# VectorE's order in the up-projections of a two-layer decoder trunk, one core of a Trainium2

## Chip, cores and metric

The kernel runs on one core of one Trainium2 chip. The metric is the time of one launch on the device in microseconds (us), the median of several runs. Its engines are TensorE (PE in the profile; its weight loads PEld), VectorE (DVE), ScalarE (ACT), GpSimd (POOL) and SyncE (SP), which issues all DMAs.

## What is computed

A residual stream `x` of 1024 tokens by 1024 features goes through two layers: gated linear attention and a gated MLP, then differential attention and a second gated MLP. The change concerns the first half of both MLPs:

```python
def conv_ffn(h, w_in, conv_w, conv_b, w_out):
    u = h @ w_in
    up = jnp.pad(u, ((0, 0), (CONV_WIDTH - 1, 0), (0, 0)))
    c = sum(up[:, j:j + S, :] * conv_w[j] for j in range(CONV_WIDTH)) + conv_b
    a, g = jnp.split(c, 2, axis=-1)
    return (jax.nn.silu(g) * a) @ w_out
```

`h` is the stream after an RMSNorm, `w_in` is 1024 by 5632, the convolution has width 3 over positions.

## The kernel before

**Numbers as pairs.** Every float32 operand of a product is split into a rounded part "hi" and the rest "lo" (`halves`, line 205): ScalarE copies hi (line 208), and VectorE subtracts to get lo (`lo_of`, line 117), which it can do only after ScalarE's copy. One 128x128 by 128x512 block product is then three matmuls: hi by hi, lo by hi, hi by lo (lines 909 to 911). An activation's pair is a tile `xp`, a weight's pair a tile `wp`.

**The up-projection.** `ffn` (from line 846, called once for each MLP) makes the 5632 columns in 22 steps `i`, each of one 128-wide block of `a` and one of `g`. A step is seven products instead of eight (a Strassen-Winograd scheme on 2 by 2 quadrants). `product(i, n)` (line 896) takes the weight pair, allots a bank of PSUM (`pf`, eight of them) and issues 12 matmuls: four k, three each. `mid(i, n, o)` (line 857) adds the result into the step's tiles `u`: mostly VectorE additions (line 114), for some n a ScalarE copy. For steps 0 and 1 some of these sums are GpSimd's (`fine(POOL, ...)`).

**Seven forms of the activations.** Each product form n has its own four `xp` tiles. Set "11" and "21" are there when `ffn` starts; "22", "t1", "t2", "t3" and "t4" are made inside it by `factor1` (line 407). The first 14 products go by n = 0, 2, 6, 4, 1, 3, 5 with i = 0 and 1 for each, and between them `factor1` is called after products 1, 2, 4, 6 and 8 (table `WHEN`). For "t1" to "t4" it does, four times over, a subtraction `h<-h` (line 114, VectorE) and then `halves` of the result: ScalarE's hi, VectorE's lo. In the text below products are counted from 0 in TensorE's order, so products 0 to 13 are steps 0 and 1, products 14 to 20 are step 2, and so on; `wp` q is the weight of product q.

**The convolution.** `conv_a(i-1)`, `conv_g0(i-1)` and `conv_g1(i-1)` are issued among the products of step i: a ScalarE start (`conv_0`, line 916), two VectorE multiply-adds of 128x1024 (`conv_1`, tile `c`), a Silu on ScalarE and a VectorE product `c<-c,c`. Step 2 carries the convolutions of steps 0 and 1.

**The weights.** `take` keeps WIN = 4 weight pairs ready ahead of the one taken. The seven weight forms of a step come from sums of its raw blocks (`sums`, line 215, and `pieces`, line 225), made by GpSimd into `wt` and `raw`, then split by `halves` into `wp`.

**Who sets the order.** TensorE, ScalarE and SyncE run in the order in which the Python code issues their instructions (`tc.manual_schedule`). VectorE's and GpSimd's order is set by the tile scheduler, which places an instruction by its own estimate of when its inputs are ready. All five run their own queue in order.

Of the kernel before, what the change touches and what calls it, by code (L numbers as in the profile page):

```python
# [28 lines left out]
NF = DFF // P  # L29
# [3 lines left out]
WIN = 4  # L33
# [4 lines left out]
WHEN = {1: "22", 2: "t1", 4: "t2", 6: "t3", 8: "t4"}  # L38
CV = (2, 3, 4, 5)
# [11 lines left out]
def trunk(  # L51
# [26 lines left out]
    PE, ACT, DVE, POOL = nc.tensor, nc.scalar, nc.vector, nc.gpsimd  # L78
# [10 lines left out]
    def uid(s):  # L89
        count[0] += 1  # L90
        return f"{s}_{count[0]}"
# [7 lines left out]
    def PS(name):  # L99
        return pp.tile([P, 512], F32, tag="p", name=uid(name))  # L100
# [9 lines left out]
    def H(hf):  # L110
        return slice(hf * HALF, (hf + 1) * HALF)

    def tt(eng, o, a, b, op):
        eng.tensor_tensor(out=o, in0=a, in1=b, op=op)  # L114
# [52 lines left out]
    LOADS, AHEAD, WENG = 3, 2, DVE  # L167
# [97 lines left out]
    def take():  # L265
        prefetch(1)
        r = ready.popleft()
        prefetch(AHEAD)
        return r
# [44 lines left out]
    def fine(eng, o, a, b, op):  # L314

        n = o.shape[-1]
        for c in range(0, n, 256 if eng is POOL else n):
            q = slice(c, c + 256 if eng is POOL else n)
            tt(eng, o[:, q], a[:, q], b[:, q], op)
# [181 lines left out]
    nm = Norm(G_ATTN0)  # L501
    X = nm.X
    tps, qps = [PS("pf"), PS("pf")], [PS("pf"), PS("pf")]
    AHEAD, LOADS = 0, 0
# [3 lines left out]
    for d in range(ND):  # L508
# [17 lines left out]
        if d == 5:  # L526
            LOADS = 3
            prefetch(0)
    AHEAD = 2
# [320 lines left out]
    def ffn(l, nm, g):  # L850
        nonlocal AHEAD
        nonlocal LOADS
        F = nm.f
        FS = ("11", "t2", "21", "t3", "t1", "t4", "22")
        up_tiles = {}

        def mid(i, n, o):

            ua, ug = up_tiles[i]
            a1, a2, g1, g2 = (t[:, 2 + q * HALF:2 + (q + 1) * HALF] for t in (ua, ug) for q in range(2))  # L860
            if i < 2:
                if n == 0:
                    ACT.activation(g1, o, AF.Copy)
                elif n == 2:
                    tt(DVE, a1, o, g1, ALU.add)
                elif n == 6:
                    ACT.activation(a2, o, AF.Copy)
                elif n == 4:
                    ACT.activation(g2, o, AF.Copy)
                    tt(DVE, a2, o, a2, ALU.add)  # L870
                elif n == 1:
                    tt(DVE, g1, o, g1, ALU.add)
                    fine(POOL, a2, a2, g1, ALU.add)
                elif n == 3:
                    tt(DVE, g1, o, g1, ALU.add)
                    fine(POOL, g2, g2, g1, ALU.add)
                else:
                    tt(DVE, g1, o, g1, ALU.add)
                return
            if n == 0:  # L880
                ACT.activation(a1, o, AF.Copy)
            elif n == 1:
                tt(DVE, a2, o, a1, ALU.add)
            elif n == 2:
                tt(DVE, a1, o, a1, ALU.add)
            elif n == 3:
                tt(DVE, g1, o, a2, ALU.add)
            elif n == 4:
                tt(DVE, g2, o, g1, ALU.add)
                tt(DVE, a2, o, a2, ALU.add)  # L890
            elif n == 5:
                tt(DVE, g1, o, g1, ALU.add)
            else:
                tt(DVE, a2, o, a2, ALU.add)

        def product(i, n):

            if n == 0:
                ut = [up.tile([P, 1026], F32, tag="u", name=uid("u")) for _ in range(2)]
                for t in ut:  # L900
                    POOL.memset(t[:, 0:2], 0.0)
                up_tiles[i] = ut
            w = take()
            o = PS("pf")
            fs = F[FS[n]]
            for k in range(ND // 2):
                wh, wl = w[:, k * P:(k + 1) * P], w[:, HALF + k * P:HALF + (k + 1) * P]
                xh, xl = fs[k][:, H(0)], fs[k][:, H(1)]
                PE.matmul(o, wh, xh, start=(k == 0), stop=False)  # L909
                PE.matmul(o, wl, xh, start=False, stop=False)  # L910
                PE.matmul(o, wh, xl, start=False, stop=(k == ND // 2 - 1))  # L911
            return o

        def conv_0(f, ut):
            c = U("c")
            ACT.activation(c, ut[:, 2:2 + S], AF.Identity, scale=cv[:, l, f, 2:3], bias=cv[:, l, f, 3:4])  # L916
            return c

        def conv_1(f, ut, c):
            stt(DVE, c, ut[:, 1:1 + S], cv[:, l, f, 1:2], c, ALU.mult, ALU.add)  # L920
            stt(DVE, c, ut[:, 0:S], cv[:, l, f, 0:1], c, ALU.mult, ALU.add)
# [3 lines left out]
        def conv_a(i):  # L925
            ca[i] = conv_0(i, up_tiles[i][0])
            conv_1(i, up_tiles[i][0], ca[i])
            up_tiles[i][0] = None

        def conv_g0(i):  # L930
            cg[i] = conv_0(NF + i, up_tiles[i][1])
            conv_1(NF + i, up_tiles.pop(i)[1], cg[i])

        def conv_g1(i):
            gt = cg.pop(i)
            ACT.activation(gt, gt, AF.Silu)  # L936
            a = ca.pop(i)
            tt(DVE, a, a, gt, ALU.mult)
            ca["m" if i % 2 == 0 else "a"] = a
            if i % 2 == 1:  # L940
                mix(i)
# [3 lines left out]
        def spill_m():  # L945
            for dst, src in spills:
                nc.sync.dma_start(dst, src.rearrange("p (n t) -> p n t", n=2) if len(dst.shape) == 3 else src)
            spills.clear()
# [23 lines left out]
        def load_w(f):  # L972
            t = (O if f % 2 else E)[f // 2] = U("wo")
            nc.sync.dma_start(t, w_out[l, f])

        def load_r(n, j):

            if (n, j) != (0, NJ - 1):
                r = rraw[n, j] = rawtile("tr")
                k = min(2, NJ - j)  # L980
                nc.sync.dma_start(r[:, 0:k * HALF].rearrange("p (e t) -> p e t", e=k), td[l][j // 2][:, SRC[n], 0:k])

        def factors(n, j):

            a, b = ((w[j][:, H(0)], w[j][:, H(1)]) if j in w else (None, None) for w in (E, O))
            if n == 0:
                x = a[0]
            elif n == 1:
                x = U("ws")[:, H(0)]
                tt(DVE, x, a[0], a[1], ALU.subtract)  # L990
            elif n == 2:
                x = a[0]
                tt(DVE, a[1], a[1], b[1], ALU.add)
                tt(DVE, x, a[1], x, ALU.subtract)
            elif n == 3:
                x = a[1]
            elif n == 4:
                x = a[0]
                tt(DVE, x, b[0], x, ALU.subtract)
                del E[j]  # L1000
            elif n == 5:
                x = b[1]
            else:
                x = b[0]
                del O[j]
            lp[n, j] = halves(x, "lp")
            rp[n, j] = halves(rraw[n, j - j % 2][:, H(j % 2)], "rp")
            if j % 2 == 1 or j == NJ - 1:
                del rraw[n, j - j % 2]
# [46 lines left out]
                sink.add(d, sl, ht[d])  # L1056

        AHEAD = WIN
        for k, (n, i) in enumerate((n, i) for n in (0, 2, 6, 4, 1, 3, 5) for i in range(2)):
            o = product(i, n)  # L1060
            if k == 0:
                nm.begin(1)
            if k == 1:
                nm.end(1)
            if k in WHEN:
                nm.factor1(WHEN[k])
            mid(i, n, o)
        for i in range(2, NF):
            for p, n in enumerate(range(7)):
                if i == NF - 1:  # L1070
                    AHEAD, LOADS = min(WIN, 6 - p), 0
                    if p > 0:
                        load_w(2 * p - 2)
                    if p in (3, 5):
                        load_r(0, p - 3)
                    if p > 4:
                        factors(0, p - 5)
                mid(i, n, product(i, n))
                if i == NF - 1:
                    del F[FS[n]]  # L1080
                if i == 2:
                    (conv_a, conv_g0, conv_g1, conv_a, conv_g0, conv_g1, lambda i: spill_m())[p](p // 3)
                    continue
                if p == CV[0]:
                    conv_a(i - 1)
                if p == CV[1]:
                    conv_g0(i - 1)
                if i < NF - 1 and p == CV[2]:
                    conv_g1(i - 1)
                if p == CV[3]:  # L1090
                    spill_m()

        steps = [(n, j) for n in range(7) for j in range(NJ)]
        nl, nf_ = 3, 1
        for g_, (n, j) in enumerate(steps):
# [28 lines left out]
            if n == 6:  # L1124
                AHEAD, LOADS = 2, 3
# [12 lines left out]
            if l == 1 and n == 6 and j == NJ - LASTF - 1:  # L1138
                for d in range(4):
                    x = ht[d][:, H(0)]  # L1140
# [28 lines left out]
    AHEAD = 2  # L1169
# [322 lines left out]
    AHEAD, LOADS = 1, 2  # L1492
# [27 lines left out]
    for s in range(-2, steps + 3):  # L1520
        a, i = divmod(s + 2, NB)
# [51 lines left out]
        if s == steps - 1:  # L1573
            AHEAD, LOADS, WENG = 1, 3, DVE
# [24 lines left out]
    AHEAD = 2  # L1599
# [96 lines left out]
```

## Time and profile before

| | us |
|---|---|
| median of 3 runs (2368.65 to 2371.49) | 2370.16 |
| the profiled execution | 2368.72 |
| its span | 2366.9 |
| TensorE busy in the span | 2314.1 (98%) |
| VectorE busy in the span | 1772.3 (75%) |
| ScalarE busy | 1042.9 (44%) |
| GpSimd busy | 852.4 (36%) |

The span runs from the first to the last instruction of the profiled execution; 1.8 us lie around it. The first up-projection runs from 442 to 985 us after the span's start, the second from 1687 to 2135. A busy share is a mean over stages. A wait of TensorE is read from the idle time before a matmul, which the trace puts down to the instruction that released it; since matmuls overlap, the stall is also read from the distance of two matmuls' starts. TensorE's clock is given as the granted share of its full rate.

### The profile page before, as it was taken

To read this page: it belongs to the slowest core of one execution; us is meant where nothing else is said; L and a number is where in the kernel's file an instruction comes from. 1 tells how busy PE (TensorE), PEld (TensorE's weight loads), DVE (VectorE), ACT (ScalarE), POOL (GpSimd) and SP (SyncE) were. 2 spreads that over 40 slices of the span, in tenths; PEclk is the share of its full clock that TensorE was granted. 3 is DMA by queue.
4 is the path that set the end of the run, shared out by engine and by line. 5 is a ranking of instruction groups with operands and counts; after the bars stand their busy time and mean duration, and the time that the engine had idled before them with its cause. 6 is when DMAs were issued, how large, how long until landed. Compare 5 with 4: busy or idle time off the path is not lost. (4 is left out here: it accounts for less than half of the span.)

```text
span 2366.9 us, 30070 instructions
## 1 busy us (share of the span) xinstructions
PE 2314.1 (98%) x10954; PEld 1874.5 (79%) x10954; DVE 1772.3 (75%) x2599; ACT 1042.9 (44%) x1866; POOL 852.4 (36%) x1002
## 2 busy tenths in 40 slices
PE   9999999999999999999999999999989999999997
PEld 7878887767888888888877888777767888888886
DVE  6554554789988889867148777767889988889865
ACT  5433342344433344544125555544344343434553
POOL 0210101167766641000005554623267666651001
PEclk9999999999999999999999999999999999999999
DMA  5012134122323248324233333522113323248423
GB/s 186 1 54 72 52 105 164 48 77 92 116 94 107 94 167 312 127 80 173 80 102 126 108 116 103 180 84 99 71 54 116 116 85 116 85 148 311 146 81 103
DMA packets 100852, 269.16 MB, mean 114 GB/s; under 512 B 10208, under 2 KB 23136, under 8 KB 100704
## 3 DMA queue, kind: packets, MB, share of 16 engines
q1 hardware_dynamic: 100704, 267.24, 32.9%
q8 instruction: 86, 1.41, 0.2%
q14 instruction: 62, 0.51, 0.1%
HBM read 183.84 MB, written 74.97 MB: 109 GB/s over the span
## 5 line engine op out<-in xcount | busy, mean ns | idle before, releaser
L910 PE MATMUL pf<-xp,wp 128*128 128x512 f32 x1232 | 488.9, 397 | 12.9 <-DVE wp L117 12.9
L909 PE MATMUL pf<-xp,wp 128*128 128x512 f32 x1232 | 487.5, 396 | 3.9 <-ACT wp L208 2.4
L911 PE MATMUL pf<-xp,wp 128*128 128x512 f32 x1232 | 487.4, 396 | 1.8 <-DVE xp L117 1.5
L910 PEld LDWEIGHTS pf<-xp,wp 128*128 128x128 f32 x1232 | 231.7, 188 | 74.6 <-DVE wp L117 21.0
L909 PEld LDWEIGHTS pf<-xp,wp 128*128 128x128 f32 x1232 | 231.8, 188 | 62.0 <-ACT wp L208 4.7
L911 PEld LDWEIGHTS pf<-xp,wp 128*128 128x128 f32 x1232 | 231.8, 188 | 59.0 <-DVE xp L117 5.6
L117 DVE SCALAR_TENSOR_TENSOR c<-u,cv,c 128x1024 f32<-128x1024 f32 x176 | 253.1, 1440 | 5.2 <-ACT c L916 5.2
L1018 PE MATMUL out<-rp,lp 128*128 128x512 f32 (+1 forms) x632 | 246.8, 390 | 2.0 <-ACT rp L208 2.0
L1020 PE MATMUL out<-rp,lp 128*128 128x512 f32 (+1 forms) x632 | 246.7, 390 | 0.0
L1019 PE MATMUL out<-rp,lp 128*128 128x512 f32 (+1 forms) x632 | 246.4, 390 | 0.0
L114 DVE TENSOR_TENSOR u<-pf,u 128x512 f32<-128x512 f32 x300 | 200.8, 681 | 17.3 <-POOL u L114 9.3
L114 POOL TENSOR_TENSOR rs_y<-rs_m,nhalf 128x4 f32<-128x4 f32 (+2 forms) x26 | 31.3, 1205 | 505.3 <-DVE rs_m L294 473.9
L117 DVE SCALAR_TENSOR_TENSOR wp<-raw,wp 128x512 fp32r<-128x512 f32 x180 | 167.5, 940 | 51.9 <-ACT wp L208 51.9
L278 PE MATMUL pf<-xh,wh 128*128 128x512 f32 x458 | 185.9, 406 | 1.1 <-ACT wh L198 1.1
L279 PE MATMUL pf<-xh,wl 128*128 128x512 f32 x458 | 180.5, 394 | 0.8 <-DVE wl L117 0.8
L280 PE MATMUL pf<-xl,wh 128*128 128x512 f32 x458 | 180.6, 394 | 0.0
L936 ACT ACTIVATE c<-c 128x1024 f32<-128x1024 f32 x44 | 46.7, 1061 | 230.6 <-DVE c L117 230.6
L1018 PEld LDWEIGHTS out<-rp,lp 128*128 128x128 f32 x632 | 119.2, 189 | 29.0 <-ACT rp L208 2.4
L1020 PEld LDWEIGHTS out<-rp,lp 128*128 128x128 f32 x632 | 119.1, 188 | 27.6 <-DVE rp L117 0.8
L1019 PEld LDWEIGHTS out<-rp,lp 128*128 128x128 f32 x632 | 119.1, 188 | 26.9
L114 POOL TENSOR_TENSOR wt<-raw 128x256 f32<-128x256 f32 x88 | 99.8, 1152 | 107.7 <-ACT xp L208 58.1
L117 DVE SCALAR_TENSOR_TENSOR wp<-wt,wp 128x512 fp32r<-128x512 f32 x128 | 122.1, 955 | 7.4 <-ACT wp L208 7.4
(256 smaller groups left out, 5067.3 us busy)
## 6 DMA issues: line engine op xcount, KB each, us to landing
raw<-in_w_in SPq DMA_DIRECT2D x88, 512.0 KB, 3.7
tr<-td SPq DMA_DIRECT2D x70, 512.0 KB, 4.0
td<-c SPq DMA_DIRECT2D x44, 512.0 KB, 2.8
wo<-in_w_out SPq DMA_DIRECT2D x44, 512.0 KB, 8.7
raw<-in_w_gla SPq DMA_DIRECT2D x24, 512.0 KB, 5.7
h<-hs SPq DMA_DIRECT2D x24, 512.0 KB, 4.5
td<-mt SPq DMA_DIRECT2D x22, 512.0 KB, 3.8
hs<-h SPq DMA_DIRECT2D x32, 256.0 KB, 2.0
```

Of the source, the lines that this page charges most:

```text
L114: eng.tensor_tensor(out=o, in0=a, in1=b, op=op)
L117: eng.scalar_tensor_tensor(out=o, in0=a, scalar=s, in1=b, op0=op0, op1=op1)
L278: PE.matmul(o, wh[:, k], xh[:, H(hf)], start=(k == 0), stop=False)
L279: PE.matmul(o, wl[:, k], xh[:, H(hf)], start=False, stop=False)
L280: PE.matmul(o, wh[:, k], xl[:, H(hf)], start=False, stop=(k == ND - 1))
L909: PE.matmul(o, wh, xh, start=(k == 0), stop=False)
L910: PE.matmul(o, wl, xh, start=False, stop=False)
L911: PE.matmul(o, wh, xl, start=False, stop=(k == ND // 2 - 1))
L936: ACT.activation(gt, gt, AF.Silu)
L1018: PE.matmul(o, wh, xh, start=(j == 0 or cut and j == NJ - LASTF), stop=False)
L1019: PE.matmul(o, wl, xh, start=False, stop=False)
L1020: PE.matmul(o, wh, xl, start=False, stop=(j == NJ - 1 or cut and j == NJ - LASTF - 1))
```

## The change

`mid` is no longer called right after its product. A list `late` holds one call back: after a product is issued, the `mid` of the product before is carried out, and the last one after the loops. Both loops stand in a block in which VectorE too runs in the order of the Python code.

```diff
+        def mids(*x):
+
+            if late:
+                mid(*late.pop())
+            late.append(x)
...
         AHEAD = WIN
-        for k, (n, i) in enumerate((n, i) for n in (0, 2, 6, 4, 1, 3, 5) for i in range(2)):
-            o = product(i, n)
...
-            mid(i, n, o)
-        for i in range(2, NF):
...
-                mid(i, n, product(i, n))
+        late = []
+        with tc.manual_schedule(engines={DVE.engine}):
+            for k, (n, i) in enumerate((n, i) for n in (0, 2, 6, 4, 1, 3, 5) for i in range(2)):
+                o = product(i, n)
...
+                mids(i, n, o)
+            for i in range(2, NF):
...
+                    mids(i, n, product(i, n))
...
+            mid(*late.pop())
```

TensorE's and SyncE's instructions stand in the same order as before. ScalarE's order differs only in the copies of a product's result, which stand one product later. VectorE's and GpSimd's differ at many places; three follow.

VectorE in the first MLP, set "t1" of `factor1` (`h<-h` is the subtraction, `xp` the lo half, `u<-pf` an addition of `mid`, `wp` a weight's lo half). Before:

```order
L114 TENSOR_TENSOR h_2965<-h_2965 128x512
L114 TENSOR_TENSOR h_2969<-h_2969 128x512
L114 TENSOR_TENSOR h_2982<-h_2982 128x512
L117 SCALAR_TENSOR_TENSOR xp_3588<-h_2965,xp_3588 128x512
L117 SCALAR_TENSOR_TENSOR xp_3592<-h_2969,xp_3592 128x512
L117 SCALAR_TENSOR_TENSOR xp_3596<-h_2982,xp_3596 128x512
L114 TENSOR_TENSOR h_3008<-h_3008 128x512
L114 TENSOR_TENSOR u_3482<-pf_3570,u_3483 128x512
L114 TENSOR_TENSOR u_3516<-pf_3607,u_3517 128x512
L117 SCALAR_TENSOR_TENSOR xp_3600<-h_3008,xp_3600 128x512
```

The same place now:

```order
L114 TENSOR_TENSOR h_2965<-h_2965 128x512
L117 SCALAR_TENSOR_TENSOR xp_3589<-h_2965,xp_3589 128x512
L114 TENSOR_TENSOR h_2969<-h_2969 128x512
L117 SCALAR_TENSOR_TENSOR xp_3593<-h_2969,xp_3593 128x512
L114 TENSOR_TENSOR h_2982<-h_2982 128x512
L117 SCALAR_TENSOR_TENSOR xp_3597<-h_2982,xp_3597 128x512
L114 TENSOR_TENSOR h_3008<-h_3008 128x512
L117 SCALAR_TENSOR_TENSOR xp_3601<-h_3008,xp_3601 128x512
L117 SCALAR_TENSOR_TENSOR wp_3605<-wt_3108,wp_3605 128x512
L114 TENSOR_TENSOR u_3484<-pf_3571,u_3485 128x512
```

Subtraction and lo half alternate now, each lo half directly behind the subtraction that feeds it; sets "t2", "t3" and "t4" read alike. Two additions of results moved behind the set.

GpSimd in the first MLP, the sums for step 2 (`wt`, `raw`) and the first addition for step 0 (`u<-u,u`). Before:

```order
L114 TENSOR_TENSOR wt_3777<-raw_3568 128x256
L114 TENSOR_TENSOR u_3482<-u_3482,u_3483 128x256 x2
L114 TENSOR_TENSOR wt_3777<-raw_3568 128x256
L114 TENSOR_TENSOR wt_3777<-wt_3777,raw_3566 128x256 x2
L114 TENSOR_TENSOR raw_3568<-raw_3566,raw_3568 128x256 x2
```

The same place now:

```order
L114 TENSOR_TENSOR wt_3776<-raw_3569 128x256 x2
L114 TENSOR_TENSOR wt_3776<-wt_3776,raw_3567 128x256 x2
L114 TENSOR_TENSOR raw_3569<-raw_3567,raw_3569 128x256 x2
L907 MEMSET u_3863 128x2
L907 MEMSET u_3864 128x2
L114 TENSOR_TENSOR u_3484<-u_3484,u_3485 128x256 x2
```

The addition stood in the middle of the sums and stands behind them now. The first sum also waits for another thing than before: its tile takes the place of one that product 10 reads, where it was one that an early copy of set "t3" reads.

VectorE in the first MLP, convolutions of steps 0 and 1 among the products of step 2 and 3. Before:

```order
L117 SCALAR_TENSOR_TENSOR c_3904<-u_3483,cv,c_3904 128x1024
L117 SCALAR_TENSOR_TENSOR wp_3908<-wt_3777,wp_3908 128x512
L117 SCALAR_TENSOR_TENSOR c_3904<-u_3483,cv,c_3904 128x1024
L114 TENSOR_TENSOR u_3862<-pf_3911,u_3862 128x512
L114 TENSOR_TENSOR u_3863<-pf_3941,u_3862 128x512
L114 TENSOR_TENSOR u_3863<-pf_3962,u_3863 128x512
L114 TENSOR_TENSOR c_3883<-c_3883,c_3904 128x1024
L117 SCALAR_TENSOR_TENSOR wp_3934<-raw_3787,wp_3934 128x512
```

The same place now:

```order
L117 SCALAR_TENSOR_TENSOR c_3905<-u_3485,cv,c_3905 128x1024 x2
L117 SCALAR_TENSOR_TENSOR wp_3909<-wt_3776,wp_3909 128x512
L114 TENSOR_TENSOR u_3863<-pf_3891,u_3863 128x512
L114 TENSOR_TENSOR c_3884<-c_3884,c_3905 128x1024
L117 SCALAR_TENSOR_TENSOR wp_3935<-raw_3786,wp_3935 128x512
```

Fewer additions of results stand ahead of a weight's lo half than before: here three came before `wp` 21 since `wp` 20, now one.

## Rows read from the trace of the kernel before

**Rows 1.** Stretches of both up-projections; columns PE, PEld, DVE, ACT, POOL busy, PEclk, DMA, GB/s.
```profile
500.00:545.00 45.00, 39.09 (x162) 29.48 (x161) 43.59 (x45) 18.90 (x26) 33.30 (x31) 1.00 0.25 88
545.00:985.00 440.00, 440.00 (x1895) 355.67 (x1894) 397.64 (x473) 186.34 (x282) 221.17 (x245) 1.00 0.40 141
...
1790.00:1840.00 50.00, 50.00 (x217) 40.44 (x216) 48.68 (x52) 20.29 (x29) 34.10 (x35) 1.00 0.28 92
```

**Rows 2.** Waits of TensorE, whole span: us in total, times, longest.
```profile
PE pf L910 <- DVE wp L117: 12.9, 12, 1.6
...
PE pf L911 <- DVE xp L117: 1.5, 4, 0.4
```

**Rows 3.** Timeline of TensorE, first up-projection: start, duration, instruction, idle before and releaser.
```profile
455.24 0.40 PE L909 MATMUL pf<-xp,wp 128*128 128x512 f32 x1
...
487.50 0.39 PE L909 MATMUL pf<-xp,wp 128*128 128x512 f32 x1
...
540.45 0.50 PE L910 MATMUL pf<-xp,wp 128*128 128x512 f32 x1 [1.35 <-DVE wp L117]
540.79 0.40 PE L911 MATMUL pf<-xp,wp 128*128 128x512 f32 x1
...
543.11 0.40 PE L909 MATMUL pf<-xp,wp 128*128 128x512 f32 x1
```

**Rows 4.** Timeline of VectorE, first up-projection, making of the activation forms.
```profile
449.89 2.72 DVE L117 SCALAR_TENSOR_TENSOR h<-h,gains_sb,rb 128x512 f32<-128x512 f32 x4 [1.15 <-PE rb L311]
...
458.17 1.89 DVE L114 TENSOR_TENSOR h<-h 128x512 f32<-128x512 f32 x3
459.98 1.89 DVE L117 SCALAR_TENSOR_TENSOR xp<-h,xp 128x512 fp32r<-128x512 f32 x3
461.78 0.69 DVE L114 TENSOR_TENSOR h<-h 128x512 f32<-128x512 f32 x1
...
482.88 1.29 DVE L117 SCALAR_TENSOR_TENSOR xp<-h,xp 128x512 fp32r<-128x512 f32 x2
```

**Rows 5.** Timeline of ScalarE: one hi copy of set "t1", one of a weight.
```profile
462.50 0.63 ACT L208 ACTIVATE xp<-h 128x512 fp32r<-128x512 f32 x1 [1.77 <-DVE h L114]
...
488.68 0.63 ACT L208 ACTIVATE wp<-wt 128x512 fp32r<-128x512 f32 x1 [4.55 <-POOL wt L114]
```

**Rows 6.** Timeline of VectorE, first up-projection, end of step 1 and steps 2 to 4.
```profile
486.60 0.69 DVE L114 TENSOR_TENSOR u<-pf,u 128x512 f32<-128x512 f32 x1 [0.63 <-POOL u L114]
489.35 1.25 DVE L117 SCALAR_TENSOR_TENSOR wp<-wt,wp 128x512 fp32r<-128x512 f32 x1 [2.05 <-ACT wp L208]
...
497.20 0.69 DVE L114 TENSOR_TENSOR u<-pf,u 128x512 f32<-128x512 f32 x1 [2.04 <-POOL u L114]
...
499.03 1.75 DVE L117 SCALAR_TENSOR_TENSOR c<-u,cv,c 128x1024 f32<-128x1024 f32 x1
...
539.17 1.23 DVE L117 SCALAR_TENSOR_TENSOR wp<-raw,wp 128x512 fp32r<-128x512 f32 x1
```

**Rows 7.** Timeline of GpSimd, first up-projection: sums for step 2, first addition.
```profile
476.49 1.66 POOL L114 TENSOR_TENSOR wt<-raw 128x256 f32<-128x256 f32 x1 [29.14 <-ACT xp L208]
483.05 3.52 POOL L114 TENSOR_TENSOR u<-u,u 128x256 f32<-128x256 f32 x2 [4.90 <-DVE u L114]
...
490.09 1.82 POOL L114 TENSOR_TENSOR u<-u,u 128x256 f32<-128x256 f32 x2
491.85 1.98 POOL L114 TENSOR_TENSOR u<-u 128x256 f32<-128x256 f32 x2
...
495.72 1.44 POOL L114 TENSOR_TENSOR u<-u 128x256 f32<-128x256 f32 x2
```

**Rows 8.** Timeline of TensorE at the start of the second up-projection.
```profile
1687.47 0.61 PE L909 MATMUL pf<-xp,wp 128*128 128x512 f32 x1 [2.41 <-ACT wp L208]
1687.87 0.63 PE L910 MATMUL pf<-xp,wp 128*128 128x512 f32 x1
1688.30 0.63 PE L911 MATMUL pf<-xp,wp 128*128 128x512 f32 x1
```

More of the change, by code (lines that the diff above doesn't have):

```diff
@@ L1058, in ffn @@
         AHEAD = WIN
-        for k, (n, i) in enumerate((n, i) for n in (0, 2, 6, 4, 1, 3, 5) for i in range(2)):
-            o = product(i, n)
[L1061 to L1066, printed above, removed]
-            mid(i, n, o)
-        for i in range(2, NF):
[L1069 to L1077, printed above, removed]
-                mid(i, n, product(i, n))
[L1079 to L1091, printed above, removed]
@@ new lines, in ffn @@
+        late = []
+        with tc.manual_schedule(engines={DVE.engine}):
+            for k, (n, i) in enumerate((n, i) for n in (0, 2, 6, 4, 1, 3, 5) for i in range(2)):
+                o = product(i, n)
+                if k == 0:
+                    nm.begin(1)
+                if k == 1:
+                    nm.end(1)
+                if k in WHEN:
+                    nm.factor1(WHEN[k])
+                mids(i, n, o)
+            for i in range(2, NF):
+                for p, n in enumerate(range(7)):
+                    if i == NF - 1:
+                        AHEAD, LOADS = min(WIN, 6 - p), 0
+                        if p > 0:
+                            load_w(2 * p - 2)
+                        if p in (3, 5):
+                            load_r(0, p - 3)
+                        if p > 4:
+                            factors(0, p - 5)
+                    mids(i, n, product(i, n))
+                    if i == NF - 1:
+                        del F[FS[n]]
+                    if i == 2:
+                        (conv_a, conv_g0, conv_g1, conv_a, conv_g0, conv_g1, lambda i: spill_m())[p](p // 3)
+                        continue
+                    if p == CV[0]:
+                        conv_a(i - 1)
+                    if p == CV[1]:
+                        conv_g0(i - 1)
+                    if i < NF - 1 and p == CV[2]:
+                        conv_g1(i - 1)
+                    if p == CV[3]:
+                        spill_m()
+            mid(*late.pop())
```

## The prediction

> **What bounds the kernel now.** I read first the busy times by stretch of the up-projections [rows 1]. From 545 us on TensorE is busy all the time (440.00 of 440 us), while VectorE has 397.64: there TensorE is the bound, nothing on VectorE is worth anything, and a reordering can only do harm. In the 103 us before, VectorE is nearly full (43.59 of 45 us between 500 and 545) and TensorE isn't (39.09). Then the waits of TensorE over the whole span [rows 2]: in up-projections it idles 12.9 us for a weight's lo half and 1.5 us for an activation's, both VectorE's. So the change acts on the first four steps of each MLP, where VectorE sets the end.
>
> How much there is to win comes from the starts of matmuls [rows 3]. Undisturbed, ten of them take 543.11 - 540.79 = 2.32 us, 0.232 each, and a product of 12 takes 2.79. Product 4 starts at 455.24, product 14 at 487.50, product 31 at 543.11. Ten products should take 27.9 us and took 32.3 (4.4 lost, stretch 1); seventeen should take 47.4 and took 55.6 (8.2 lost, stretch 2). That is 12.6 us for each MLP. The second has the same pattern, and no more than 25 us are there for the taking.
>
> **Part 1: subtraction and lo half alternate (stretch 1).** VectorE works without a gap from 449.89 to 484.17, the end of the last xp lo half [rows 4], and product 12 ends on it. Three subtractions take 1.81 us from first start to next start (458.17 to 459.98), so an operation costs 0.60. Before, three subtractions ran in a row, and ScalarE's copies fell behind the next ones. Now the lo half stands directly behind its subtraction, and in VectorE's own queue it holds up everything until ScalarE has copied. The round trip from rows: the subtraction lasts 0.69 (461.78 to 462.47), ScalarE starts 0.03 later and takes 0.63 [rows 4, 5]; from ScalarE's end to VectorE's start it is 0.04 (488.68 + 0.63 = 489.31, then 489.35) [rows 5, 6]. So the lo half starts 0.69 + 0.03 + 0.63 + 0.04 = 1.39 after its subtraction, where 0.60 would do: 0.79 lost. Four sets of four make 16 x 0.79 = **12.6 us** for each MLP. No cover exists: what could run in the gap stands behind in the same queue.
>
> Check by counting: VectorE now has 8 gain multiplications (0.66 each from 449.89 on, four in 2.64) and 46 operations of 0.60 up to the last lo half, 5.3 + 27.7 = 33.0 us; with 12.6, and 0.4 twice where a weight's copy follows the last activation copy on ScalarE, it ends at 496.3 instead of 484.17. The lo half of weight 13 and an addition come behind it now; product 13 waits for that, ends 12.7 later than before, and product 14 starts at about 500.2.
>
> Deferring the results takes two additions, 1.2 us, from in front of the last lo half (in the count). The result copies on ScalarE stand one product later; their banks come free later, but there are eight banks and only one more is held: I cost that at nothing. SyncE's queue is unchanged.
>
> **Part 2: GpSimd's sums.** Before, the first addition for step 0 stood amid the sums for step 2 and waited 4.90 us for VectorE [rows 7], and VectorE then stood still for GpSimd or for the copies of its sums: 0.63 + 2.05 + 2.04 us and more [rows 6]. Now the sums come first, which ends the 2.05. But they now wait for product 10, which ends at about 486.4, so they start 10 us later than at 476.49 and fall into the gaps of set "t4". A lo half beside GpSimd's work took 1.25 instead of 0.68 [rows 4, 6]; six such pieces cost VectorE between nothing and 6 x 0.57 = 3.4 us. I take **1.0**: a gap of 0.79 just holds one piece (1.44 for two when undisturbed [rows 7]).
>
> The four additions and the sum between them remain a chain, each waiting for VectorE and VectorE's next for it. The addition of product 8 comes at 497.4. Before, the chain ran from 483.05 to 497.16, with other work between; its own pieces are 3.52 + 1.82 + 1.98 + 1.44 = 8.8 us [rows 7], and about 2 for the sum between them (as the pieces beside it), 10.8 us. At that pace it ends at 508, undisturbed (about 0.72 a piece, 7.2 us) at 505.3. So the convolution, which started at 499.03 [rows 6], starts between 505 and 509.4; I take 508.2, **9.2 later**, near the upper end since VectorE is full then.
>
> **Part 3: convolution and weights (stretch 2).** From 499.03 to the lo half of weight 30 (539.17 + 1.23 = 540.40) VectorE took 41.4 us [rows 6], almost without a gap, and product 30's second matmul at 540.45 waits for it [rows 3]. The operations up to there are the same now, less two additions (1.2 us) that moved behind. So weight 30 is ready at 508.2 + 40.2 = 548.4, 549.4 with part 2's 1.0. TensorE, starting product 14 at 500.2, could be there at 545.1 at the earliest, so VectorE still decides: 8.0 to 9.0 later than before. Of the 12.7 lost in stretch 1 some 4 come back, as stalls of stretch 2 that TensorE no longer has. After that TensorE is the bound, and the lag stays to the end.
>
> **Sum.** 8.5 us for each MLP, 17 for both. Against the profiled execution, 2368.72 + 17 = 2385.7 (span 2366.9 + 17 = 2384). The median of the runs shown is 1.4 above that execution; I say **2386**. The bounds: if stretch 2 stalls nowhere, 545.1 - 540.45 = 4.6 each, 9 for both, 2378. If GpSimd disturbs by the full 3.4 and its chain is at the slow end (509.4 - 499.03 - 1.2 = 9.2), 12.6 each, 25 for both, 2394.
>
> **Rivals.**
> *Faster.* The gain of order: weights stand ahead of results, GpSimd's sums unblocked, all of stretch 2's 8.2 back. Then the sign hangs on one number, the wait at a lo half in set "t1" to "t4": 16 waits against 8.2 us, so it turns at 8.2 / 16 = 0.51 us a wait. If ScalarE's copy were hidden altogether, the time is 2368.7 - 2 x (8.2 + 1.2) = 2350. For it: [rows 2] name just these waits. Against: ScalarE's copy alone lasts 0.63 [rows 5], and nothing can be put before it in an in-order queue.
> *No change.* That 0.51 is met, or the order printed isn't what binds there: 2369 to 2372. It needs the same short wait; and the order shows that the change does what it says.
> *Falls behind everywhere.* In its fullest 50 us VectorE has 48.68 busy, beside a full TensorE [rows 1]. If fixed order costs 1 us more in each of the 18 later steps (c<-c,c behind the Silu, say), the lead of four weights is eaten and TensorE waits: up to 36 us, 2404 to 2420. Against: over 440 us VectorE has 42 spare, and weights now stand ahead of results.
> *TensorE's clock.* In stretch 1 TensorE will get three matmuls in 2 us, then a gap, sixteen times in each MLP. In the rows its clock fell after an idle time of 2.41 us: matmuls then start 0.43 apart, 1.2 GHz instead of 2.4 [rows 8]; with idle times up to 1.35 [rows 3] it stayed at 1.00 [rows 1]. A fall in stretch 1 would be hidden behind VectorE (a product takes 5.1 us, two 10.3, and a set 9.6); only its tail counts, some eight matmuls by 0.2, 1.6 us for each MLP: 2389.
> The Trainium skill, "TensorE: Matmul & The Clock Gate", section "A second HAM failure mode: psum-queue depth-cycling", says that short idle times between groups of matmuls, if frequent, make the clock go back and forth. By that rule the fall is to be expected here; the trace before, full rate in 500 to 545 despite such idle times, does not show it.
>
> **Chances.** The forecast (2378 to 2394) 0.75; clock 0.08; falling behind 0.07; no change 0.05; faster 0.05. The range 2377 to 2399 holds the first two and the unknown costs. Slower than 0.2% (4.7 us, about what a measurement tells from no change) takes the first three: 0.90; same 0.05; faster 0.05.
>
> **What would show it.** After the change: in the timeline of VectorE, single subtractions 1.99 us apart with lo halves between them that idle 0.7 for ScalarE, 16 in each MLP; TensorE waiting for xp (hi and lo) some 10 us an MLP or more instead of 1.5 in all; product 14 near 500; the convolution near 508; TensorE without a gap from step 5 on, shifted by 8 to 9. Wrong if those lo halves idle under 0.5, if product 14 starts before 495, or if TensorE has waits later than step 5.

## The result and the profile after

The changed kernel takes 2389.05 us (median of 6 runs, 2385.22 to 2391.85), the one before 2370.83 in the runs beside it: 18.2 us slower, ratio 1.0075, 95% interval 1.0065 to 1.0086. The forecast was 2386, with 2377 to 2399 as range.

The profiled execution of the changed kernel took 2385.22 us (span 2383.2), 16.5 more than that of before. Part of such a difference is chance: across all the profiled kernels of this study the first matmul of the first up-projection starts anywhere between 442.07 and 445.28, though the code ahead of it is the same. So stages are compared by their own length, from the first to the last start of a matmul of the up-projection: 443.68 us before (442.07 to 885.76) and 452.48 after in the first MLP, 445.29 and 453.72 in the second. That is 8.80 and 8.43 us, 17.2 together. (The first up-projection ends at 885.76, not at 985, as the text ahead of the prediction has it; its row of 545 to 985 us runs into the next stage. From 545 to 885.76 TensorE has 340.76 us busy and VectorE 308.62, so TensorE was full there all the same, and VectorE had 32 to spare, not 42.)

The waits of TensorE over the whole span, both MLPs together (us in total, times, longest), to be set beside [rows 2]:

```profile
PE pf L915 <- ACT xp L208: 14.2, 18, 1.4
...
PE pf L916 <- DVE wp L117: 1.8, 4, 0.9
...
PE pf L917 <- DVE xp L117: 0.4, 1, 0.4
```

The 12.9 us for a weight's lo half have become 1.8. In their place stand 14.2 for an activation's hi half, where the kernel before had this:

```profile
PE pf L909 <- ACT xp L208: 1.2, 2, 0.6
```

ScalarE is named, as it comes last, but it is VectorE that keeps ScalarE: the timeline of VectorE in sets "t1" and "t4" of the first MLP shows how (start, duration, instruction, idle before and releaser).

```profile
451.07 2.72 DVE L117 SCALAR_TENSOR_TENSOR h<-h,gains_sb,rb 128x512 f32<-128x512 f32 x4 [1.38 <-PE rb L311]
...
459.35 0.68 DVE L114 TENSOR_TENSOR h<-h 128x512 f32<-128x512 f32 x1
460.73 0.69 DVE L117 SCALAR_TENSOR_TENSOR xp<-h,xp 128x512 fp32r<-128x512 f32 x1 [0.70 <-ACT xp L208]
461.34 0.68 DVE L114 TENSOR_TENSOR h<-h 128x512 f32<-128x512 f32 x1
462.73 0.69 DVE L117 SCALAR_TENSOR_TENSOR xp<-h,xp 128x512 fp32r<-128x512 f32 x1 [0.70 <-ACT xp L208]
...
489.58 1.23 DVE L114 TENSOR_TENSOR h<-h,h 128x512 f32<-128x512 f32 x1
491.56 1.08 DVE L117 SCALAR_TENSOR_TENSOR xp<-h,xp 128x512 fp32r<-128x512 f32 x1 [0.76 <-ACT xp L208]
492.57 1.22 DVE L114 TENSOR_TENSOR h<-h,h 128x512 f32<-128x512 f32 x1
...
498.64 0.69 DVE L117 SCALAR_TENSOR_TENSOR xp<-h,xp 128x512 fp32r<-128x512 f32 x1 [0.76 <-ACT xp L208]
499.25 0.68 DVE L114 TENSOR_TENSOR u<-pf,u 128x512 f32<-128x512 f32 x1
...
500.45 0.68 DVE L114 TENSOR_TENSOR u<-pf,u 128x512 f32<-128x512 f32 x1
```

Subtractions start 1.99 us apart (459.35, 461.34) where [rows 4] had 0.60, and each lo half starts 1.38 after its subtraction, 0.70 of it idle. At 489.58 to 492.57 three operations take 1.23, 1.08 and 1.22 instead of 0.69: GpSimd's sums for step 2 run beside them. The groups of VectorE's instructions between 457 and 500 us count the waits of the first MLP (busy us and mean ns, then the idle time before them):

```profile
L117 DVE SCALAR_TENSOR_TENSOR xp<-h,xp 128x512 fp32r<-128x512 f32 x16 | 11.5, 717 | 11.5 <-ACT xp L208 11.5
```

Sixteen lo halves, 11.5 us of idle time. Then, from the timeline of TensorE, the starts of products 4, 13, 14 and 31, the second matmul of product 30 (550.44), and the one wait from product 14 on that is over half a microsecond (weight 23):

```profile
456.42 0.40 PE L915 MATMUL pf<-xp,wp 128*128 128x512 f32 x1
...
500.10 0.63 PE L915 MATMUL pf<-xp,wp 128*128 128x512 f32 x1
...
504.21 0.40 PE L915 MATMUL pf<-xp,wp 128*128 128x512 f32 x1
...
530.65 0.50 PE L916 MATMUL pf<-xp,wp 128*128 128x512 f32 x1 [0.92 <-DVE wp L117]
...
550.44 0.49 PE L916 MATMUL pf<-xp,wp 128*128 128x512 f32 x1
...
553.10 0.40 PE L915 MATMUL pf<-xp,wp 128*128 128x512 f32 x1
```

This execution reached product 0 at 443.26, 1.19 later than that of before, so 1.19 is taken off in every comparison with it. Product 14 comes 504.21 - 487.50 - 1.19 = 15.5 later [rows 3], product 31 comes 553.10 - 543.11 - 1.19 = 8.8 later: seventeen products took 48.9 us instead of 55.6, against 47.4 without a stall. Nearly seven of the fifteen came back as stalls that TensorE no longer has.

VectorE again, at the end of GpSimd's chain, the first convolution and the lo half of weight 30:

```profile
508.82 0.69 DVE L114 TENSOR_TENSOR u<-pf,u 128x512 f32<-128x512 f32 x1 [2.03 <-POOL u L114]
...
511.36 3.52 DVE L117 SCALAR_TENSOR_TENSOR c<-u,cv,c 128x1024 f32<-128x1024 f32 x2
...
549.15 1.23 DVE L117 SCALAR_TENSOR_TENSOR wp<-raw,wp 128x512 fp32r<-128x512 f32 x1
```

And GpSimd's chain (to be set beside [rows 7]):

```profile
488.09 2.16 POOL L114 TENSOR_TENSOR wt<-raw 128x256 f32<-128x256 f32 x2 [39.20 <-PE pf L917]
...
501.21 4.26 POOL L114 TENSOR_TENSOR u<-u,u 128x256 f32<-128x256 f32 x4 [5.22 <-DVE u L114]
505.43 1.97 POOL L114 TENSOR_TENSOR wt<-raw,wt 128x256 f32<-128x256 f32 x2
507.35 3.37 POOL L114 TENSOR_TENSOR u<-u 128x256 f32<-128x256 f32 x4
```

The sums start on product 10's end, 488.09 - 476.49 - 1.19 = 10.4 us later than before, and the additions follow at 501.21. Last, the stretches of [rows 1] again (columns as there), ahead of them the longest of the three stretches of the first up-projection in which the granted clock was 0.50:

```profile
495.92:502.75 6.83, 5.74 (x12) 3.69 (x13) 5.41 (x9) 4.86 (x9) 1.61 (x3) 0.50 0.11 38
...
500.00:545.00 45.00, 44.08 (x183) 34.70 (x183) 40.83 (x45) 19.16 (x26) 34.29 (x32) 0.97 0.28 97
545.00:985.00 440.00, 440.00 (x1896) 355.48 (x1895) 386.89 (x471) 187.64 (x279) 248.67 (x257) 1.00 0.40 142
...
1790.00:1840.00 50.00, 50.00 (x217) 40.16 (x216) 47.79 (x51) 21.90 (x31) 44.02 (x42) 1.00 0.36 127
```

Between 500 and 545 TensorE has 44.08 busy now instead of 39.09, and VectorE 40.83 instead of 43.59. From 545 on TensorE is full, as before.

### The profile page after: what moved, and what is told of

The parts are those of the page before. It is cut to its first block, busy times and chain, and to the rows that moved or that the text cites. A ratio compares the mean times of both kernels' runs of the same rounds, so it can differ in the third digit from the quotient of the medians.

```text
span 2383.2 us, 30074 instructions
## 1 busy us (share of the span) xinstructions
PE 2329.3 (98%) x10954; PEld 1881.7 (79%) x10954; DVE 1748.7 (73%) x2599; ACT 1046.3 (44%) x1866; POOL 889.0 (37%) x1002
## 5 line engine op out<-in xcount | busy, mean ns | idle before, releaser
L915 PE MATMUL pf<-xp,wp 128*128 128x512 f32 x1232 | 493.6, 401 | 16.8 <-ACT xp L208 14.2
L916 PE MATMUL pf<-xp,wp 128*128 128x512 f32 x1232 | 493.4, 400 | 1.9 <-DVE wp L117 1.8
L917 PE MATMUL pf<-xp,wp 128*128 128x512 f32 x1232 | 493.6, 401 | 0.4 <-DVE xp L117 0.4
L915 PEld LDWEIGHTS pf<-xp,wp 128*128 128x128 f32 x1232 | 234.7, 191 | 79.7 <-ACT xp L208 22.4
L917 PEld LDWEIGHTS pf<-xp,wp 128*128 128x128 f32 x1232 | 234.6, 190 | 62.8 <-DVE xp L117 9.6
L916 PEld LDWEIGHTS pf<-xp,wp 128*128 128x128 f32 x1232 | 234.6, 190 | 61.8 <-DVE wp L117 8.1
L114 DVE TENSOR_TENSOR u<-pf,u 128x512 f32<-128x512 f32 x300 | 201.4, 682 | 30.0 <-PE pf L917 22.8
L117 DVE SCALAR_TENSOR_TENSOR wp<-raw,wp 128x512 fp32r<-128x512 f32 x180 | 160.5, 893 | 7.3 <-ACT wp L208 7.3
L114 POOL TENSOR_TENSOR wt<-raw,wt 128x256 f32<-128x256 f32 x80 | 97.1, 1236 | 150.0 <-DVE wp L117 150.0
L117 DVE SCALAR_TENSOR_TENSOR wp<-wt,wp 128x512 fp32r<-128x512 f32 x128 | 97.3, 760 | 59.1 <-ACT wp L208 59.1
```

Of the source, the lines that this page charges most:

```text
L117: eng.scalar_tensor_tensor(out=o, in0=a, scalar=s, in1=b, op0=op0, op1=op1)
```

## Experiments

Three theories were set against each other. **Theory 1**: the loss is the wait of each lo half for ScalarE's copy, 16 times in each MLP. **Theory 2**: it is GpSimd's later sums and the fixed order of weights and results behind product 14. **Theory 3**: it is TensorE's lower clock. All times stand beside runs of the kernel before on the same chip.

The table gathers what was measured: the median and the ratio to before, and from the profiled execution of each the time of products 2 to 14, of 14 to 31 (first MLP), and the length of both up-projections.

| kernel | us | ratio, 95% interval | 2 to 14 | 14 to 31 | up-projections |
|---|---|---|---|---|---|
| before | 2370.83 | 1 | 37.9 | 55.6 | 443.7, 445.3 |
| changed | 2389.05 | 1.0075 (1.0065 to 1.0086) | 53.4 | 48.9 | 452.5, 453.7 |
| front_only | 2392.42 | 1.0097 (1.0083 to 1.0111) | 53.8 | 52.7 | 456.7, 456.3 |
| late_only | 2363.09 | 0.9968 (0.9955 to 0.9980) | 37.9 | 52.4 | 440.4, 441.9 |
| defer_only | 2370.70 | 1.0000 (0.9991 to 1.0009) | 37.9 | 56.6 | 444.7, 446.7 |
| grouped | 2361.18 | 0.9964 (0.9951 to 0.9976) | 41.4 | 49.7 | 441.3, 442.5 |
| half_rows | 2374.33 | 1.0013 (1.0004 to 1.0022) | 45.7 | 49.8 | 445.6, 446.9 |
| nodefer | 2389.52 | 1.0080 (1.0066 to 1.0094) | 54.5 | 49.5 | 454.1, 455.4 |
| filler | 2386.93 | 1.0068 (1.0055 to 1.0082) | 52.6 | 49.7 | 452.5, 453.9 |
| rows_sched | 2367.12 | 0.9984 (0.9975 to 0.9992) | 37.8 | 54.9 | 443.0, 444.1 |
| rows_dve_sums | 2359.90 | 0.9952 (0.9940 to 0.9965) | 42.4 | 47.4 | 440.0, 441.4 |
| late_dve_sums | 2358.22 | 0.9952 (0.9938 to 0.9965) | 40.5 | 47.4 | 438.2, 439.4 |

### The waits taken away: grouped

```diff
-            for d in range(n):
-                if x is not None:
-                    tt(DVE, to[d], x[d], y[d], ALU.subtract)
+            if x is not None:
+                for d in range(n):
+                    tt(DVE, to[d], x[d], y[d], ALU.subtract)
+            for d in range(n):
                 self.f[q].append(halves(to[d], "xp"))
```

> The changed kernel with the four subtractions of a set t1 to t4 in a row and the four lo halves behind them; all else in program order, results one product later. Theory 1 (the wait of each lo half for ScalarE's copy, 16 x 0.70 us in each MLP, is the loss): the 0.70 us waits vanish, the last xp lo half of the first MLP ends near 486 instead of 499.33, product 14 starts near 489 instead of 504.21, and the time falls below that of the kernel before, to between 2356 and 2370, since the idle time of VectorE between 484 and 499 is still gone. Theory 2 (GpSimd's sums, now behind product 10, and the fixed order of weights and results from product 14 on are the loss): the waits vanish as well, but the time stays at 2380 or above. Theory 3 (TensorE's lower clock is the loss): the clock stays up here as TensorE no longer stops 16 times, so this run does not tell it from theory 1.

It took 2361.18 us. Against the changed kernel 27.9 us are gone, by moving three lines. The groups of VectorE's instructions between 457 and 488 us:

```profile
L117 DVE SCALAR_TENSOR_TENSOR xp<-h,xp 128x512 fp32r<-128x512 f32 x16 | 10.5, 717 | 0.0
L114 DVE TENSOR_TENSOR h<-h,h 128x512 f32<-128x512 f32 x12 | 9.6, 863 | 0.0
```

The same 16 lo halves idle 0.0 now, while GpSimd's later sums, the order behind product 14 and the deferral are all still in. Theory 2 asked for 2380 or more and falls. Product 14 came at 491.79, 2.8 later than the 489 expected; the mean of 863 ns, where an undisturbed subtraction takes 0.69 us, points at why, and the last part of this section takes it up.

### The first 14 products and the rest apart: front_only, late_only, defer_only

Each keeps the deferral; only the extent of the block of program order differs. The edit of late_only:

```diff
-        with tc.manual_schedule(engines={DVE.engine}):
+        if True:
             for k, (n, i) in enumerate((n, i) for n in (0, 2, 6, 4, 1, 3, 5) for i in range(2)):
...
+        with tc.manual_schedule(engines={DVE.engine}):
             for i in range(2, NF):
```

front_only closes the block ahead of the second loop instead, and defer_only has no block.

> Program order for VectorE only from product 14 on (steps 2 to 21), the first 14 products as the scheduler orders them; results one product later everywhere. Theory 1: stretch 1 is that of the kernel before (product 14 near 488.5), stretch 2 loses less than 8.2 us because weights stand ahead of results; 2356 to 2371. Theory 2: 2380 or above, since all that it blames is in. Theory 3: clock as before, 2356 to 2371, no difference to theory 1.

> Program order for VectorE only in the first 14 products, the scheduler's order after; results one product later everywhere. Theory 1: 16 waits of 0.70 us are there, product 14 starts near 504; time as changed or above, 2385 to 2396. Theory 2: the loss is gone but for the later sums, 2369 to 2376. Theory 3: as theory 1.

> The scheduler's order for VectorE throughout, with the results alone asked for one product later. If the gain that remains when the waits are taken away comes from fixed program order, this is the kernel before: 2367 to 2373. If it comes from the deferral, 2358 to 2364.

The first two came out as theory 1 said, and defer_only is the kernel before, so the deferral has no part in it. Program order in the first 14 products costs 2392.42 - 2370.70 = 21.7 us, or 2389.05 - 2363.09 = 26.0 with program order behind it too. Program order behind them gains 7.6 us alone (2370.70 to 2363.09) and 3.4 with the other (2392.42 to 2389.05). So the change is a loss and a smaller gain, in different places. The waits of TensorE in front_only:

```profile
PE pf L915 <- ACT xp L208: 16.1, 20, 1.4
PE pf L916 <- DVE wp L117: 6.0, 5, 2.3
```

and in late_only:

```profile
PE pf L916 <- DVE wp L117: 8.1, 12, 1.1
...
PE pf L915 <- ACT xp L208: 1.2, 2, 0.6
```

Each loss shows where its order stands: hi halves 16.1 us with program order at the front and 1.2 without, weights 8.1 with program order behind and 12.9 before [rows 2].

### Half the waits: half_rows

```diff
+            row = q in ("t1", "t2")
+            for d in range(n if row else 0):
+                tt(DVE, to[d], x[d], y[d], ALU.subtract)
             for d in range(n):
-                if x is not None:
+                if x is not None and not row:
                     tt(DVE, to[d], x[d], y[d], ALU.subtract)
```

> The changed kernel with the subtractions of sets t1 and t2 in a row, those of t3 and t4 still alternating with their lo halves: 8 waits of 0.70 us in each MLP instead of 16. If every wait counts the same to the end, the time lies midway between 2361 (none) and 2389 (sixteen): 2375, say 2372 to 2378. If the later sets' waits count more, since the earlier ones can be made up by the time of set t4, 2379 or above; if the gain of order swallows the first ten waits, as the prediction's turning point of 0.51 us a wait says, 2370 or below.

2374.33, within 1 us of the midpoint. The groups between 457 and 500 us:

```profile
L117 DVE SCALAR_TENSOR_TENSOR xp<-h,xp 128x512 fp32r<-128x512 f32 x19 | 12.8, 706 | 5.9 <-ACT xp L208 5.9
```

5.9 us idle instead of 11.5, and half the loss: from 0 to 16 waits each costs about (2389.05 - 2361.18) / 32 = 0.87 us, a little more than its 0.70 of idle time. The turning point that the prediction gave for its rival "faster" is thereby refuted: with 8 waits of some 0.74 us, 5.9 in all and less than 8.2, the kernel should have gained, and it is 3.4 us slower than before (ratio 1.0013, just clear of 1). Products 2 to 14 lose 7.8 us to these waits and what falls into them, and the order behind gives back 5.8 (table).

### The deferral taken away: nodefer

```diff
-                mids(i, n, o)
+                mid(i, n, o)
...
-                    mids(i, n, product(i, n))
+                    mid(i, n, product(i, n))
...
-            mid(*late.pop())
```

> The changed kernel without the deferral: each product's result is asked for right behind it, all else in program order. In sets t1 to t4 VectorE then stands until the second product of a set has ended before it begins the next set: about 2.8 us for each of three or four sets, on top of the 16 waits. Product 14 later than 504 by 8 to 12 us, the time 2400 to 2415. If results asked for late cost something of their own (banks, the sums on GpSimd), the run would instead be at 2389 or below.

2389.52: the same as the changed kernel, and the expectation of 2400 to 2415 was wrong. It took the result that stands ahead of a set for that of a product which needs the set before. But `factor1` is called four products ahead of a set's first use ("t1" after product 2, for product 6), so between two sets stand results of products that had ended by then: from 455 to 506 us VectorE has no wait for a matmul. Further on it does wait for products:

```profile
DVE u L114 <- PE pf L917: 64.1, 66, 1.5
```

In the changed kernel the same group has 22.8 us (28 times). The 41.3 us more of waits cost nothing that the times show: TensorE is the bound there, and VectorE stands behind it.

### The clock held up: filler

```diff
                 PE.matmul(o, wl, xh, start=False, stop=False)
+                if i == 0 and n in (4, 1, 3, 5):
+                    for _ in range(3):
+                        PE.matmul(o, wl, xh, start=False, stop=False)
```

> The changed kernel, with three more matmuls (the wl times xh one repeated) ahead of the wh times xl one of each triple in products 6, 8, 10 and 12: 48 in each MLP, which run in TensorE's waits; the up-projections of four products come out with the lo term of the weight four times. It keeps TensorE at work while VectorE stands. Theory 3: the clock stays at full rate up to product 13, product 13 takes 2.8 us instead of 3.9, and the time falls by 4 us or more, to 2384 or below. Theory 1: VectorE's lo half of weight 23 and 30 set the end, and what TensorE wins comes back as a wait there: 2385 to 2390, a gain of 0 to 3 us; if the extra matmuls only delay the triples, up to 2393.

From 455 to 505 us, first filler, then the changed kernel (columns as in [rows 1]):

```profile
455.00:505.00 50.00, 45.56 (x182) 32.82 (x181) 37.20 (x57) 20.56 (x36) 9.59 (x12) 1.00 0.08 22
```

```profile
455.00:505.00 50.00, 41.92 (x131) 26.87 (x130) 37.08 (x56) 20.70 (x37) 10.26 (x12) 0.86 0.07 22
```

The extra matmuls keep the granted clock at 1.00 instead of 0.86, and the up-projections take 452.53 and 453.91 us, against 452.48 and 453.72. The medians differ by 2.1 us with intervals that overlap widely. The low clock was there and cost nothing that can be told from zero: products 2 to 14 took 52.6 us instead of 53.4, and products 14 to 31 took 49.7 instead of 48.9. What TensorE won, it waited for VectorE a few products later, at weights 22 and 23:

```profile
526.69 0.50 PE L916 MATMUL pf<-xp,wp 128*128 128x512 f32 x1 [0.32 <-DVE wp L117]
...
530.87 0.50 PE L916 MATMUL pf<-xp,wp 128*128 128x512 f32 x1 [1.15 <-DVE wp L117]
```

### What is left of stretch 1 and of GpSimd's chain: rows_sched, rows_dve_sums, late_dve_sums

rows_sched has the edit of grouped in the kernel before, so the scheduler orders VectorE. The other two put `mid`'s additions for steps 0 and 1 on VectorE, in grouped and in late_only:

```diff
-                    fine(POOL, a2, a2, g1, ALU.add)
+                    tt(DVE, a2, a2, g1, ALU.add)
...
-                    fine(POOL, g2, g2, g1, ALU.add)
+                    tt(DVE, g2, g2, g1, ALU.add)
```

> The kernel before, with the subtractions of a set in a row and the lo halves behind, in the program alone: the scheduler still orders VectorE, and results are asked for at once. If the rows take away waits that the scheduler's order had already avoided, nothing changes: 2368 to 2373. If rows by themselves are the gain of the kernel with rows in program order, 2358 to 2364.

> The kernel with all four sets' subtractions in a row, and the four additions of two results (steps 0 and 1) on VectorE instead of GpSimd. In the run of the first that changed rows VectorE stood 0.63 + 0.64 + 2.03 = 3.3 us for GpSimd there; four additions on VectorE cost 4 x 0.6 = 2.4. 0.9 us less for each MLP, and up to 2 with what GpSimd's own use of the port cost: 2357 to 2361 against 2361. If the convolution's start isn't what sets weights 23 and 30, no change.

> Program order only from product 14 on, with the four additions of two results on VectorE instead of GpSimd. The first 14 products took 37.87 us from product 2 on under the scheduler's order against 41.4 to 42.5 with rows in program order, but there the next 17 still lost 5 us to VectorE. If the additions shorten VectorE's work there as they did with rows (2.3 us less in stretch 2 of the first MLP), each up-projection loses 2 us less than with program order from product 14 on alone: 2357 to 2360 against 2363. If VectorE's total work sets the end whatever the order, it comes out with rows and additions on VectorE, 2359 to 2361.

rows_sched gains 0.16% (0.08 to 0.25%), between the two ranges expected: rows are a small gain by themselves, not the 9.3 us of grouped. It also shows what GpSimd's sums can do to VectorE. The four subtractions of set "t4" on VectorE, first in rows_sched, then in grouped:

```profile
479.89 2.49 DVE L114 TENSOR_TENSOR h<-h,h 128x512 f32<-128x512 f32 x4
```

```profile
479.20 4.64 DVE L114 TENSOR_TENSOR h<-h,h 128x512 f32<-128x512 f32 x4
```

Same instructions, 2.15 us more. GpSimd's sums for step 2 run beside them in both kernels; what differs is who waits. GpSimd beside these subtractions, rows_sched first:

```profile
479.32 6.05 POOL L114 TENSOR_TENSOR wt<-raw 128x256 f32<-128x256 f32 x1
```

```profile
479.84 2.32 POOL L114 TENSOR_TENSOR wt<-wt,raw 128x256 f32<-128x256 f32 x2
482.12 2.31 POOL L114 TENSOR_TENSOR raw<-raw,raw 128x256 f32<-128x256 f32 x2
```

In rows_sched a single sum lasted 6.05 us while VectorE ran at full pace, and VectorE stood 3.52 us for a GpSimd addition later (at 490.70). In grouped both advanced together, at about 1.2 us for each operation, where alone a sum takes about 0.7 and a subtraction 0.69. Why it went one way here and the other way there, these runs do not show. With the two lo halves next to them (1.09 us, and four in 3.01 instead of 2.49) VectorE lost about 3.1 us there, most of why grouped needs 41.4 us for products 2 to 14 where the scheduler's order needs 37.9.

With the additions on VectorE, products 14 to 31 take 47.4 us in both kernels: no stall is left behind product 14. In late_dve_sums TensorE is busy throughout the stretch:

```profile
500.00:545.00 45.00, 45.00 (x196) 36.29 (x195) 44.79 (x47) 20.69 (x28) 35.56 (x33) 1.00 0.30 100
```

The profiled up-projections shorten by 1.1 to 1.3 us from grouped and by 2.2 to 2.5 from late_only. The medians, 2359.90 and 2358.22, lie 1.3 and 4.9 us under those of the kernels they come from, but the intervals of the ratios overlap both times, so the gain rests on the profiled executions. Both beat the kernel before and the changed one; late_dve_sums has the lowest median, 12.5 us under before, and cannot be told from rows_dve_sums by its ratio.

## Why the prediction was right

**Direction and size.** Forecast was 17 us more, 8.5 in each MLP; the up-projections are 8.80 and 8.43 longer in the profile, and the medians differ by 18.2 (15 to 20 by the interval). The 2386 is 17 added to the profiled execution; added to the median of that time, 2370.16, it gives 2387.2.

**The round trip, part 1: right.** 1.39 us from subtraction to lo half was worked out and 1.38 measured; the pairs are 1.99 apart where two operations of 0.60 need 1.20, which is the 0.79 forecast, 16 times in each MLP. grouped, half_rows and late_only show that this is the cause, each in its own way. That nothing covers the wait in this order was right too. One of its signs did not come: TensorE was to wait some 10 us in each MLP for `xp`, and its idle time there is 14.2 + 0.4 in both together, 7.3 each. Part of the loss stands as busy time instead, as between 495.92 and 502.75, where TensorE is busy 5.74 of 6.83 us at a clock of 0.50.

**Product 14: too early.** Forecast 12.7 later, measured 15.5. Two amounts are missing, both seen. Three operations of set "t4" ran beside GpSimd's sums and took 0.54 + 0.39 + 0.53 = 1.5 us more; part 2 had put 1.0 for this, but only on weight 30 and not on product 14. And product 13 took 4.1 us, from 500.10 to 504.21, instead of 2.8: the clock was at 1.2 GHz until 502.75, the rival "TensorE's clock" happening inside the forecast case. Most of that 1.3 is the clock's: in filler, at full rate, product 13 takes 3.07. 12.7 + 1.5 + 1.3 = 15.5.

**GpSimd's chain: right in length, late in start.** From the addition of product 8 to the convolution 10.8 us were forecast and 511.36 - 500.45 = 10.9 taken (the additions at 499.25 and 500.45 are those of products 7 and 8). But it came at 500.45 - 1.19 = 499.3 instead of 497.4, as the last lo half of set "t4" did (498.64 + 0.69 - 1.19 = 498.1 instead of 496.3). So the convolution started at 511.36 - 1.19 = 510.2, beyond the forecast 505 to 509.4. (Those bounds are loose: the 508 counts the chain from the start of the addition of product 8, the 505.3 from its end, and the 509.4 has no working.) The step that failed is again the 1.0 for GpSimd's sums, which belonged in front of the chain.

**Weight 30: right by two errors that cancel.** From the convolution to the end of that lo half 40.2 us were assumed, and 549.15 + 1.23 - 511.36 = 39.0 taken. So it is ready at 550.38 - 1.19 = 549.2, between the forecast 548.4 and 549.4, and 8.8 later than before.

**Who decides then: half right.** VectorE was to be the one at weight 30. TensorE wanted it at 550.44, 0.06 after it was ready: a tie. The last real stall was at weight 23 (0.92 us idle), from where TensorE ran on. TensorE was 4.1 later than the 545.1 forecast, by the 1.5 + 1.3 above, this stall and 0.4 of smaller ones, which is why the clock cost nothing in the end: without its loss the lo halves would have been waited for, as filler shows.

**What costs nothing: right.** The deferral alone is 2370.70 against 2370.91 (defer_only), and its removal changes nothing (nodefer); the banks held longer were not felt.

**The rivals.** "Faster" named the right gain, weights ahead of results, and its lever, the wait at each lo half; without the waits it is 2361, not the 2350 worked out: in grouped products 14 to 31 still lose 2.3 us, and products 2 to 14 take 3.5 more than before, about 3.1 of it beside GpSimd's sums. Its turning point of 0.51 us was too high, as half_rows shows. "Falls behind everywhere" did not come: TensorE had 440.00 of 440 us from 545 on. The clock did fall, to 0.50 from 468.61, 478.85 and 495.92 us on, and was hidden. That the measured 2389 is that rival's figure is chance: with the clock held up the up-projections are as long. Its own numbers did not hide a fall throughout, since two products at the low clock (10.3 us) take longer than a set (9.6); but the first two falls lasted 3.4 us each and the third 6.8. The Trainium skill ("TensorE: Matmul & The Clock Gate", section "A second HAM failure mode: psum-queue depth-cycling") has the rule that frequent short idle times between groups of matmuls make the clock go back and forth. The 0.86 of the changed kernel against the 1.00 of filler agrees with it.

## What to carry to other kernels

When an engine is put into program order, read the program for pairs in which its second instruction needs another engine's answer to the first: each pair costs the part of the round trip that its own work does not fill (here 0.79 of 1.39 us), times its count, and a loop split into two (all first halves, then all second halves) gives it back. The scheduler had hidden that, so a fixed order must write the interleaving out by hand; the same program order was a gain behind product 14 (late_only). Time each stretch from its own first to its own last matmul, since what a stretch loses the next one can give back: here 15.5 us lost became 8.8.

## What was not expected

TensorE's clock fell to 1.2 GHz in the changed kernel after idle times of at most 1.4 us for an activation; before, waits of up to 1.6 us had left it at 2.4 [rows 1, 2]. Here they followed one another, about 2 us apart with three matmuls between them, but that need not be what decides: in rows_sched the clock fell at 511.67, right after a single idle time of 1.62, and one of the same length at 510.98 in the kernel before was followed by no fall. What decides stays open. And the fall did not matter. Extra matmuls put into those gaps held the clock at 1.00.

Four VectorE subtractions of 128x512 took 4.64 us where they and GpSimd's sums advanced together, and 2.49 where a sum of GpSimd's was held up beside them for 6.05. Rows of single operations had shown only 1.25 against 0.69.
